# Sums of output weight blocks made in memory during attention, in a hybrid attention and gated-linear-attention block

## The chip, the cores and the metric

The kernel runs on one core of one Trainium2 chip. The metric is device time in microseconds (us). A core has TensorE (PE in the profile, with its weight loads as PEld), VectorE (DVE), ScalarE (ACT), GpSimd (POOL) and SyncE (SP); SP and POOL also issue DMAs, each on a queue of its own, and all DMAs run on the core's 16 DMA engines.

## What is computed

```python
h = rms_norm(x) * (1.0 + scale) + shift            # x: 512 x 2048, float32
proj = h @ w_in                                    # 2048 -> 7200 columns
aq, ak, av, ag, gq, gk, gv, gg, lr_f, lr_b = split(proj)
...                                                # dilated attention, 16 heads x 64, times silu(ag)
...                                                # gated linear attention, 4 heads, times silu(gg)
y = concatenate([a_out, g_out]) @ w_out            # 512 x 2048 @ 2048 x 2048
x = x + gate * y
return rms_norm(x) * final_gain
```

All is float32. A matrix product is made of three passes of TensorE on halves of each operand: a high half (rounded by ScalarE, lines 403 and 1094) and a low half (what is left, by VectorE, lines 389 and 1095); the passes are high x high, low x high and high x low (`three`, lines 213 to 215).

## The kernel before, in words

The work goes in stages. Up to about 188 us the condition vector, the normalised input and the first products are made. Then come ten "units", each a product of h with 512 columns of w_in in eight groups of 24 matmuls: qk2, qk4, qk6, gk, gv0, gv1, ag0, ag1, gg0, gg1. Each group's weights (128 x 1024, 512 KB) are loaded by SP into one of four `raw` buffers (`fetch`). Between a unit's matmuls stands other work, placed by a fraction of the unit: attention for two pairs of heads in each of qk2, qk4, qk6 and gk, the linear attention's heads in gv1, ag0, ag1 and gg0. A tile of attention goes from scores on TensorE (line 691) over VectorE, ScalarE and POOL (normalisation of p, line 703) back to TensorE (transposition, line 715). Where a pair of heads begins, parts of its keys (tiles ks and kl) are copied to the other half of the partitions by SP's DMAs (lines 664, 666); each head's bias (tile g) is loaded from memory too (line 679).

The order of TensorE's instructions is the program's. Those of the other engines are ordered, when the program is built, by a scheduler that takes what it holds ready, by priority; work placed between the matmuls has a raised priority. On the chip each engine's queue is in order: an instruction that waits holds those behind it.

The output projection multiplies by blocks in the manner of Winograd's form of Strassen: w_out's 2048 columns are taken as two pairs of 512-column halves (`OUT_PAIRS`), and each pair needs seven products of half size instead of eight, in the order P1, P7, P6, P4, P5, P3, P2. A product has four steps g of 12 matmuls, each with a 512 KB block of weights O0, O1, ... (28 for each pair, 56 in all). Four of the seven need sums (or with them sums of sums) of weight blocks: with blocks "11", "21", "12", "22", P7 takes T3 = 12 + 22, P6 takes T2 = 11 + 12 + 22, P4 takes T4 = T2 + 21, P5 takes T1 = 11 + 12. Before the change, `out_fetch` loads "12" into one of four `sum` tiles and has POOL issue an accumulating DMA that adds "22" from memory into it; after P7's use the same tile gets "11" added for P6, and after that "21" for P4. P5 loads a `raw` tile and adds to it. Weights are fetched two to four steps ahead. The operands' sums and halves are made beside it (`halves`, `to_s1` to `to_s4`), and `keep` and `add_up` take the products out.

Of the kernel before, what the change touches and what calls it, by code (L numbers as in the profile page):

```python
# [10 lines left out]
F32 = mybir.dt.float32  # L11
# [3 lines left out]
ALU = mybir.AluOpType  # L15
# [3 lines left out]
P = 128  # L19
# [60 lines left out]
def _runs():  # L80
# [6 lines left out]
    for j in range(2):  # L87
        cols = np.arange(512 * j, min(512 * j + 512, NREL))
        part = []
        for b, v in enumerate(seen):  # L90
            c = cols[bucket[cols] == v] - 512 * j
            if len(c):
# [24 lines left out]

OUT_ORDER = ("P1", "P7", "P6", "P4", "P5", "P3", "P2")
OUT_PAIRS = ((0, 1), (3, 2))
OUT_WEIGHTS = {"P1": ("11", None), "P7": ("12", "22"), "P6": (None, "11"), "P4": (None, "21"),  # L120
               "P5": ("11", "12"), "P3": ("22", None), "P2": ("21", None)}


def _plan(tasks, free, ready):
# [52 lines left out]
def block_kernel(ctx: ExitStack, tc: tile.TileContext, a: dict):  # L177
    nc = tc.nc
# [9 lines left out]
    dp = ctx.enter_context(tc.tile_pool(name="dp", bufs=1, space=DRAM))  # L188
# [8 lines left out]
    def PJ(name):  # L197
        return pp.tile([P, 512], F32, tag="pj", bufs=5, name=name)
# [13 lines left out]
    def three(ps, lh, ll, rh, rl, first, last, more=False):  # L212
        mm(ps, lh, rh, start=first, stop=False, skip_group_check=more)  # L213
        mm(ps, ll, rh, start=False, stop=False, skip_group_check=more)  # L214
        mm(ps, lh, rl, start=False, stop=last, skip_group_check=more)  # L215
# [27 lines left out]
    def RAW(name, shape):  # L243
        return wp.tile([P] + shape, F32, tag="raw", bufs=4, name=name)
# [100 lines left out]
    groups = [(u, g) for u in order for g in range(KT // 2)]  # L345
    groups += [("O", s) for s in range(2 * 4 * len(OUT_ORDER))]
    gi = {ug: i for i, ug in enumerate(groups)}
    raws, wts, low, sums_of = {}, {}, set(), {}

    def fetch(i):  # L350
        if i < len(groups) and i not in raws:
            u, g = groups[i]
            if u == "O":
                raws[i] = out_fetch(g)
            else:
                raws[i] = RAW(f"raw_{u}{g}", [2, 512])
                nc.sync.dma_start(raws[i], a["w_" + u][g])

    def out_fetch(s):

        pair, q = divmod(s, 4 * len(OUT_ORDER))
        prod, g = OUT_ORDER[q // 4], q % 4
        l, r = OUT_PAIRS[pair]
        block = {"11": (l, g), "21": (l, 4 + g), "12": (r, g), "22": (r, 4 + g)}
        load, add = OUT_WEIGHTS[prod]
        if load is None:
            t = sums_of[g]
        elif prod == "P7":
            t = sums_of[g] = op.tile([P, 2, 512], F32, tag="sum", bufs=4, name=f"sum{pair}{g}")
        else:  # L370
            t = RAW(f"raw_O{s}", [2, 512])
        if load is not None:
            j, z = block[load]
            nc.sync.dma_start(t, a[f"w_o{j}"][z])
        if add is not None:
            j, z = block[add]
            nc.gpsimd.dma_start(t, a[f"w_o{j}"][z], accum_op=ALU.add)  # L377
        return t

    def split(i):  # L380
        split_hi(i)
        split_lo(i)

    def split_lo(i):
        if i in raws and i not in low:
            u, g = groups[i]
            raw = raws[i].rearrange("p k c -> p (k c)")
            hi, lo = wts[i]
            tt(lo, raw, hi.bitcast(F32), op=ALU.subtract)
            low.add(i)  # L390

    def split_hi(i):
        if i < len(groups) and i not in wts:
            fetch(i)
            u, g = groups[i]
            raw = raws[i].rearrange("p k c -> p (k c)")
            dst = None
            if (u, g) == ("O", len(groups) - gi["O", 0] - 4):
                t = b8.tile([P, 2, 1024], F32R, tag="b8", name="wlast")
                dst = t[:, 0, :], t[:, 1, :]  # L400
            wts[i] = dst or (wp.tile([P, 1024], F32R, tag="whi", name=f"{u}{g}h"),
                             wp.tile([P, 1024], F32R, tag="wlo", name=f"{u}{g}l"))
            act(wts[i][0], raw, AF.Copy)
# [150 lines left out]
    for z in range(2):  # L554
        c = slice(512 * z, 512 * z + 512)
# [25 lines left out]
    n = len(chain) // 2  # L581
# [4 lines left out]
    for z in range(2):  # L586
        for e in range(3):
            name = ("mm", "a", 0, 7) if (z, e) == (1, 2) else ("m0", z, e)
# [3 lines left out]
    for i in range(n):  # L592
        if i > 7:
            mm_task(i)
        st, k, j = chain[i]
# [15 lines left out]
    for i in range(n, 2 * n):  # L611
        mm_task(i)
        st, k, j = chain[i]
# [3 lines left out]
    for w in range(4):  # L617
        for kt in range(4):
            j, g = w // 2 * 4 + kt, w % 2
# [342 lines left out]
    def urgent(go):  # L962
        with tc.high_priority(offset=20):
            go()

    spill = []

    def unit(name, natural, side=(), lr=None):
        side = sorted(spill + list(side), key=lambda x: x[0])
        spill[:] = [(at - 1, go) for at, go in side if at >= 1]  # L970
        side = [x for x in side if x[0] < 1]
        ps = [PJ(f"ps_{name}_{i}") for i in range(4)]
        pos, tick, ticks = 0, 0, 64
        for g in range(KT // 2):
            i0 = gi[name, g]
            split_hi(i0)
            split_hi(i0 + 1)
            for ahead in (2, 3):
                fetch(i0 + ahead)
            split_lo(i0)  # L980
            hi, lo = wts[i0]
            for i in range(4):
                for kk in range(2):
                    k = 2 * g + kk
                    rh, rl = h_hi[:, k, :], h_lo[:, k, :]
# [33 lines left out]
    for n, p in (("qk2", 0), ("qk4", 2), ("qk6", 4)):  # L1019
        ps = unit(n, False, attention((p, p + 1)) + ([(0.05, shift_row)] + some_sums(n) if p == 4 else []))  # L1020
        for q in range(2):
            qk_evict(p + 2 + q, ps[2 * q], ps[2 * q + 1])

    ps = unit("gk", False, attention((6, 7)) + some_sums("gk"))
    gla["k"] = B8("gkt", [4, 512])
    for i in range(4):
# [53 lines left out]
    def part(z, c):  # L1080

        return cat[z][:, :, half[c]]
# [6 lines left out]
    def halves(name, z, src):  # L1089

        hi, lo = (t[:, 4 * z:4 * z + 4, :] for t in ops[name])

        def go():
            act(hi, src, AF.Copy)
            tt(lo, src, hi.bitcast(F32), op=ALU.subtract)
        return go
# [4 lines left out]
    def diff(z):  # L1101
        d = gp.tile([P, 4, 256], F32, tag="g", name=f"diff{z}")
        tt(d, part(z, 0), part(z, 1), op=ALU.subtract)
        halves("S3", z, d)()

    def to_s1(z):
        tt(part(z, 1), part(2 + z, 1), part(z, 1), op=ALU.subtract)

    def to_s2(z):
        stt(part(z, 0), part(z, 1), -1.0, part(z, 0), op0=ALU.mult, op1=ALU.subtract)  # L1110

    def to_s4(z):
        tt(part(z, 0), part(2 + z, 0), part(z, 0), op=ALU.add)

    side = [(0.05, halves("A11", 0, part(0, 0))), (0.2, halves("A11", 1, part(1, 0))),
            (0.35, lambda: diff(0)), (0.5, lambda: diff(1)),
            (0.65, lambda: to_s1(0)), (0.8, lambda: to_s2(0))]
# [5 lines left out]
    op = ctx.enter_context(tc.tile_pool(name="op", bufs=1, reuse_waits="tile"))  # L1123
    for e in "hl":
        t = hp.tile([P, KT, 512], F32R, tag="h", name="c_" + e)
# [112 lines left out]
    def product(pair, prod, ps, first, last, rows=(0, 1)):  # L1238

        ah, al = ops[with_[prod]]  # L1240
        for g in range(4):
            s = (pair * len(OUT_ORDER) + OUT_ORDER.index(prod)) * 4 + g
            i0 = gi["O", s]
            ahead = 0 in rows
            if ahead:
                split_hi(i0)
                split_hi(i0 + 1)
                for n in (2, 3, 4):
                    fetch(i0 + n)
                split_lo(i0)  # L1250
                for go in todo.get((pair, prod, g), ()):
                    go()
            wh, wl = wts[i0]
            for n in rows:
                t = slice(P * n, P * n + P)
                for kk in range(2):
                    k = 2 * g + kk
                    c = slice(512 * kk, 512 * kk + 512)
                    three(ps[n], ah[:, k, t], al[:, k, t], wh[:, c], wl[:, c],
                          first and k == 0, last and k == 7, not first)  # L1260
                if ahead and n == 0:
                    split_lo(i0 + 1)
# [18 lines left out]
    for pair, (l, r) in enumerate(OUT_PAIRS):  # L1281
# [28 lines left out]
        s = [first_squares(n, [0, 1, r]) for n in range(2)]  # L1310
# [78 lines left out]
```

## Time and profile before

| | |
|---|---|
| median of 3 runs | 967.18 us (965.24 to 967.81) |
| profiled execution | 969.8 us, its span 968.0 us |
| mean granted TensorE clock | 0.984 |
| PE busy | 929.5 us (96%) |
| DVE, ACT, POOL busy | 656.0, 470.7, 85.7 us |
| attention (first scores to last tiles) | about 194 to 450 us |
| output projection (first matmul to last) | 768.7 to 958.4 us |
| read from and written to memory | 175.36 MB, 4.28 MB |

The rows of the profile name what an instruction writes and reads (out<-in), with its line; `sum<-in_w_o` is a load or an accumulating DMA of a weight block, `O4h` the high half of step 4's weights. A time of a wait is put to what came last. Slices are fortieths of the span, with busy shares in tenths.

### The profile page before, as it was taken

To read this page: it belongs to the slowest core of one execution; us is meant where nothing else is said; L and a number is where in the kernel's file an instruction comes from. 1 tells how busy PE (TensorE), PEld (TensorE's weight loads), DVE (VectorE), ACT (ScalarE), POOL (GpSimd) and SP (SyncE) were. 2 spreads that over 40 slices of the span, in tenths; PEclk is the share of its full clock that TensorE was granted. 3 is DMA by queue.
4 is the path that set the end of the run, shared out by engine and by line. 5 is a ranking of instruction groups with operands and counts; after the bars stand their busy time and mean duration, and the time that the engine had idled before them with its cause. 6 is when DMAs were issued, how large, how long until landed. Compare 5 with 4: busy or idle time off the path is not lost.

```text
span 968.0 us, 12067 instructions
## 1 busy us (share of the span) xinstructions
PE 929.5 (96%) x4375; PEld 763.7 (79%) x4375; DVE 656.0 (68%) x960; ACT 470.7 (49%) x770; POOL 85.7 (9%) x120
## 2 busy tenths in 40 slices
PE   8999999999999999999999999999999978898895
PEld 6888888888888888888778888888788855676684
DVE  8987999666665777666346575867875455594386
ACT  5543533655555556555135453635542444453464
POOL 0000000022121021120000000000100122102101
PEclk9999999999999999999999999999999989999898
DMA  9999596533432644534453353445444599979863
GB/s 354 401 413 374 198 349 228 157 117 104 128 104 75 196 156 136 162 107 142 145 170 112 107 167 134 156 156 170 152 153 138 174 265 250 270 249 242 173 200 148
DMA packets 51523, 184.62 MB, mean 191 GB/s; under 512 B 6436, under 2 KB 6724, under 8 KB 47240
## 3 DMA queue, kind: packets, MB, share of 16 engines
q1 hardware_dynamic: 46352, 166.44, 49.3%
q0 software_dynamic: 4672, 16.84, 8.9%
q8 instruction: 34, 0.56, 0.2%
q10 hardware_dynamic: 440, 0.57, 0.2%
q14 instruction: 25, 0.20, 0.1%
HBM read 175.36 MB, written 4.28 MB: 186 GB/s over the span
## 4 chain that ended last, share of the span: by engine, by line
PE 78%; DMA 9%; DVE 6%; issue 4%; ACT 2%; POOL 1%; SPq 0%; ACTq 0%; DVEq 0%; POOLq 0%
DMA sum<-in_w_o 5%; PE ps_qk L213 5%; PE ps_qk L215 5%; PE ps_qk L214 5%; PE o L729 3%; PE stb L215 3%; PE ps_gv L215 3%; PE ps_gv L214 3%; PE ps_gv L213 3%; PE stb L214 3%; PE t L715 3%; PE stb L213 3%; PE ps_ag L215 3%; PE ps_ag L213 3%; PE ps_ag L214 3%
## 5 line engine op out<-in xcount | busy, mean ns | idle before, releaser
L312 DVE CUSTOM_DVE_ANT_0 cb<-cb,sb,c_bcond 128x2048 f32<-128x2048 f32 (+1 forms) x32 | 73.4, 2294 | 1.0 <-DMA cb<-in_wm 0.6
L698 ACT ACTIVATE p<-p,st 128x512 f32<-128x512 f32 x64 | 46.1, 721 | 55.2 <-DVE st L695 54.8
L703 POOL TENSOR_SCALAR p<-p,st 128x512 f32<-128x512 f32 x62 | 43.0, 694 | 332.6 <-DVE st L699 283.8
L720 DVE TENSOR_TENSOR pt<-t,pt 128x512 fp32r<-128x512 f32 x64 | 43.7, 689 | 15.7 <-ACT pt L719 15.3
L695 DVE CUSTOM_DVE_ANT_0 p<-s,g 128x512 f32<-128x512 f32 x64 | 43.6, 687 | 15.2 <-PE s L692 14.9
L719 ACT ACTIVATE pt<-t 128x512 fp32r<-128x512 f32 x64 | 37.8, 591 | 9.7 <-PE t L715 8.6
L715 PEld LDWEIGHTS t<-c_ident,p 128*128 128x128 f32 x256 | 31.5, 140 | 9.7 <-POOL p L703 1.4
L715 PE MATMUL t<-c_ident,p 128*128 128x128 f32 x256 | 38.5, 273 | 0.1
L729 PEld LDWEIGHTS o<-pt,vv 128*128 128x128 f32 x256 | 34.8, 188 | 2.8
L729 PE MATMUL o<-pt,vv 128*128 128x256 f32 x256 | 35.6, 281 | 0.0
L312 DVE CUSTOM_DVE_ANT_0 rawg<-rawg,sb,gate 128x1024 f32<-128x1024 f32 x16 | 20.5, 1282 | 15.8 <-DMA rawg<-in_wg 15.7
L891 POOL TENSOR_SCALAR dc<-st,sc 128x256 f32<-128x256 f32 x16 | 8.5, 530 | 253.0 <-DVE st L888 248.1
L377 POOL DMA_DIRECT2D sum<-in_w_o x24 | 21.5, 919 | 67.4 <-DMA sum<-in_w_o 38.6
L699 DVE RECIPROCAL st<-st 128x1 f32<-128x1 f32 x64 | 10.3, 161 | 24.9 <-ACT p L698 24.9
L312 DVE CUSTOM_DVE_ANT_0 rawg<-rawg,sb,c_bcond 128x1024 f32<-128x1024 f32 x16 | 20.5, 1280 | 6.9 <-DMA rawg<-in_wg 6.9
L692 PE MATMUL s<-kl,qs 128*128 128x512 f32 x64 | 25.0, 391 | 0.0
L691 PE MATMUL s<-ks,qs 128*128 128x512 f32 x64 | 25.0, 390 | 0.0
L898 ACT ACTIVATE sq<-st,sc 128x256 f32<-128x256 f32 x24 | 12.2, 507 | 18.6 <-DVE st L888 10.4
L732 ACT ACTIVATE oh<-o 64x256 f32<-64x256 f32 x32 | 12.2, 381 | 14.4 <-PE o L729 13.4
L312 DVE CUSTOM_DVE_ANT_0 rawv<-rawv,shb,vbias 128x1024 f32<-128x1024 f32 x8 | 10.6, 1324 | 12.6 <-DMA rawv<-in_wv 12.6
L736 DVE TENSOR_TENSOR cat<-o,oh 64x256 f32<-64x256 f32 x32 | 13.3, 416 | 8.2 <-ACT oh L732 7.8
L467 ACT ACTIVATE h_hi<-xt,shift 128x512 fp32r<-128x512 f32 x16 | 11.5, 719 | 13.0 <-DVE shift L312 13.0
(1520 smaller groups left out, 2984.1 us busy)
## 6 DMA issues: line engine op xcount, KB each, us to landing
cb<-in_wm SPq DMA_DIRECT2D x31, 1024.0 KB, 8.9
rawg<-in_wg SPq DMA_DIRECT2D x32, 512.0 KB, 3.3
raw_O<-in_w_o SPq DMA_DIRECT2D x32, 512.0 KB, 4.8
raw_qk<-in_w_qk SPq DMA_DIRECT2D x24, 512.0 KB, 3.3
sum<-in_w_o POOLq DMA_DIRECT2D x24, 512.0 KB, 11.9
rawb<-in_w_sb SPq DMA_DIRECT2D x16, 512.0 KB, 5.4
rawv<-in_wv SPq DMA_DIRECT2D x16, 512.0 KB, 4.0
raw_gv<-in_w_gv SPq DMA_DIRECT2D x16, 512.0 KB, 3.3
```

Source lines behind the costliest of these rows:

```text
L213: mm(ps, lh, rh, start=first, stop=False, skip_group_check=more)
L214: mm(ps, ll, rh, start=False, stop=False, skip_group_check=more)
L215: mm(ps, lh, rl, start=False, stop=last, skip_group_check=more)
L312: nc.vector.tensor_tensor_reduce(out=w, in0=w, in1=with_, op0=ALU.mult, op1=ALU.add, scale=1.0, scalar=init, accum_out=dst)
L691: mm(ps, qs[:, q], ks, start=True, stop=False)
L695: nc.vector.tensor_tensor_reduce(out=t, in0=ps, in1=gt[h][:, P * i:P * i + 512], op0=ALU.add, op1=ALU.min, scale=1.0, scalar=3e38, accum_o ...
L698: act(t, t, AF.Exp, bias=st[:, 0:1], scale=-1.0, accum_out=st[:, 1:2])
L703: nc.gpsimd.tensor_scalar(t, t, st[:, 2:3], 1.0, op0=ALU.mult, op1=ALU.mult)
L715: nc.tensor.transpose(pk[:, kt * P:kt * P + P], t[:, kt * P:kt * P + P], ident)
L719: act(hi, src, AF.Copy)
L720: tt(lo, src, hi.bitcast(F32), op=ALU.subtract)
L729: mm(po[:, :256], vv[h // 4][:, kt, h % 4, :], t[:, w, kt, :], start=kt == 0 and w == 0, stop=kt == 3 and w == 1)
```

## The change

The sums are made in memory. For each pair and step g there are four tiles of 512 KB in memory: T1, T3, T2 and T4 (`OUT_SUMS`). Each is made by a copy from memory to memory, issued by SP (`sum_start`: a block of w_out, or T1 for T2, or T2 for T4), and an accumulating DMA, issued by POOL (`sum_add`), that adds another block in memory: 32 copies and 32 adds in 64 rows of 8 KB. A copy of T2 or T4 waits for the add that finishes its source, and an add waits for its copy. `block_sums` hands the 64 operations out to the ten units by `SUM_OPS_IN`, in the order of a pipeline of six stages, placed evenly in each unit with raised priority.

The output projection then loads every block plainly: 56 loads by SP, none by POOL. The four `sum` tiles are gone; odd steps from 7 on use three buffers of their own, the others the four `raw` buffers, and loads are fetched two to five steps ahead.

```diff
-OUT_WEIGHTS = {"P1": ("11", None), "P7": ("12", "22"), "P6": (None, "11"), "P4": (None, "21"),
-               "P5": ("11", "12"), "P3": ("22", None), "P2": ("21", None)}
+OUT_WEIGHTS = {"P1": "11", "P7": "T3", "P6": "T2", "P4": "T4", "P5": "T1", "P3": "22", "P2": "21"}
+OUT_SUMS = {"T1": ("11", "12"), "T3": ("12", "22"), "T2": ("T1", "22"), "T4": ("T2", "21")}
+OUT_DEEP = 6
+SUM_OPS_IN = {"qk2": 7, "qk4": 7, "qk6": 7, "gk": 7, "gv0": 5, "gv1": 7, "ag0": 7, "ag1": 6, "gg0": 6, "gg1": 5}
...
     def out_fetch(s):
...
-        if load is None:
-            t = sums_of[g]
-        elif prod == "P7":
-            t = sums_of[g] = op.tile([P, 2, 512], F32, tag="sum", bufs=4, name=f"sum{pair}{g}")
+        if s % 2 and s >= OUT_DEEP:
+            t = op.tile([P, 2, 512], F32, tag="raw", bufs=3, name=f"raw_O{s}")
         else:
             t = RAW(f"raw_O{s}", [2, 512])
-        if load is not None:
-            j, z = block[load]
-            nc.sync.dma_start(t, a[f"w_o{j}"][z])
-        if add is not None:
-            j, z = block[add]
-            nc.gpsimd.dma_start(t, a[f"w_o{j}"][z], accum_op=ALU.add)
+        if what in OUT_SUMS:
+            d = dsum[pair, what, g]
+            nc.sync.dma_start(t.rearrange("p k c -> p (k c)"),
+                              bass.AP(d.tensor, d.offset, [[1024, P], [1, 1024]]))
+        else:
+            nc.sync.dma_start(t, out_block(pair, what, g))
         return t
...
+    def flat(t):
+        return bass.AP(t.tensor, t.offset, [[2048, 64], [1, 2048]])
+
+    def sum_start(pair, name, g):
+        def go():
+            src = OUT_SUMS[name][0]
+            dsum[pair, name, g] = t = dp.tile([64, 2048], F32, tag=f"{name}{pair}{g}", name=f"{name}{pair}{g}")
+            nc.sync.dma_start(t, flat(dsum[pair, src, g] if src in OUT_SUMS else out_block(pair, src, g)))
+        return go
+
+    def sum_add(pair, name, g):
+        def go():
+            nc.gpsimd.dma_start(dsum[pair, name, g], flat(out_block(pair, OUT_SUMS[name][1], g)), accum_op=ALU.add, max_dma_last_dim=8192)
+        return go
+
+    sum_ops = []
+    for s in range(13):
+        for lag, fn, name in ((0, sum_start, "T1"), (0, sum_start, "T3"), (1, sum_add, "T1"), (1, sum_add, "T3"),
+                              (2, sum_start, "T2"), (3, sum_add, "T2"), (4, sum_start, "T4"), (5, sum_add, "T4")):
+            if 0 <= s - lag < 8:
+                sum_ops.append(fn(*[((s - lag) // 4), name, (s - lag) % 4]))
+
+    def block_sums(name):
+        n = SUM_OPS_IN[name]
+        r = [sum_ops.pop(0) for _ in range(n)]
+        return [((q + 0.5) / n, x) for q, x in enumerate(r)]
...
-        side = sorted(spill + list(side), key=lambda x: x[0])
+        side = sorted(spill + list(side) + block_sums(name), key=lambda x: x[0])
...
-                for n in (2, 3, 4):
+                for n in (2, 3, 4, 5):
                     fetch(i0 + n)
```

TensorE's instructions and their order are the same. Three places show how the others stand now. The first is SP's queue in the unit qk2, where weights of the next unit (raw_qk4..), the heads' biases (g2 to g5) and, now, the copies are issued; a name such as T201 is sum T2 of pair 0, step 1. Before:

```order
L679 DMA g2_1706<-grow_149 128x896
L357 DMA raw_qk41_1983<-in_w_qk4 128x1024
L679 DMA g3_1846<-grow_149 128x896
L357 DMA raw_qk42_2067<-in_w_qk4 128x1024
L357 DMA raw_qk43_2173<-in_w_qk4 128x1024
L679 DMA g4_2164<-grow_149 128x896
```

and now:

```order
L711 DMA g2_1712<-grow_149 128x896
L392 DMA T200_2472<-T100_1554 16x8192
L392 DMA T103_2583<-in_w_o0 16x8192
L359 DMA raw_qk41_1992<-in_w_qk4 128x1024
L392 DMA T303_2679<-in_w_o1 16x8192
L711 DMA g3_1854<-grow_149 128x896
L392 DMA T201_2942<-T101_1707 16x8192
L359 DMA raw_qk42_2077<-in_w_qk4 128x1024
L392 DMA T110_3148<-in_w_o3 16x8192
L392 DMA T310_3259<-in_w_o2 16x8192
L359 DMA raw_qk43_2185<-in_w_qk4 128x1024
L711 DMA g4_2176<-grow_149 128x896
```

Six copies stand between loads that followed each other; T200 and T201 read what an add has finished, so SP waits for it there, with the loads behind. The second place is POOL in the same unit, where the probabilities of each tile (p10 is tile 0 of head 1) are normalised. Before:

```order
L703 TENSOR_SCALAR p10_1668<-p10_1668,st10_1669 128x512
L703 TENSOR_SCALAR p11_1711<-p11_1711,st11_1712 128x512
L703 TENSOR_SCALAR p12_1739<-p12_1739,st12_1740 128x512
L703 TENSOR_SCALAR p13_1780<-p13_1780,st13_1781 128x512
L703 TENSOR_SCALAR p20_1802<-p20_1802,st20_1803 128x512
```

and now:

```order
L735 TENSOR_SCALAR p10_1672<-p10_1672,st10_1673 128x512
L397 DMA T302_2215<-in_w_o1 64x2048
L735 TENSOR_SCALAR p11_1717<-p11_1717,st11_1718 128x512
L397 DMA T200_2472<-in_w_o1 64x2048
L735 TENSOR_SCALAR p12_1745<-p12_1745,st12_1746 128x512
L397 DMA T103_2583<-in_w_o1 64x2048
L735 TENSOR_SCALAR p13_1786<-p13_1786,st13_1787 128x512
L397 DMA T303_2679<-in_w_o1 64x2048
L735 TENSOR_SCALAR p20_1808<-p20_1808,st20_1809 128x512
```

An accumulating DMA now stands ahead of nearly every normalisation, and waits for its copy to land. By the order all 64 operations are in the attention units: the first copy stands before the first bias g0, the last, of T413, before the load of qk66, and its add before p90, though the code hands them out up to gg1. The third place is SP's queue at the start of the output projection. Before:

```order
L374 DMA raw_O2_6404<-in_w_o0 128x1024
L374 DMA raw_O3_6462<-in_w_o0 128x1024
L374 DMA raw_O16_6715<-in_w_o0 128x1024
L374 DMA raw_O17_6736<-in_w_o0 128x1024
L374 DMA sum00_6464<-in_w_o1 128x1024
L374 DMA sum01_6485<-in_w_o1 128x1024
L1137 DMA garow_6492<-gatet_6490 16x128
L374 DMA sum02_6511<-in_w_o1 128x1024
```

and now:

```order
L380 DMA raw_O2_6499<-in_w_o0 128x1024
L380 DMA raw_O3_6558<-in_w_o0 128x1024
L377 DMA raw_O4_6560<-T300_1610 128x1024
L377 DMA raw_O5_6562<-T301_1814 128x1024
L377 DMA raw_O7_6607<-T303_2679 128x1024
L1169 DMA garow_6588<-gatet_6586 16x128
L377 DMA raw_O9_6651<-T201_2942 128x1024
L377 DMA raw_O6_6582<-T302_2215 128x1024
```

Where two loads for P5 stood early and the sums' first parts followed, the finished sums T3 (for O4 to O7) and T2 (O8 on) are loaded in their turn.

More of the change, by code (lines that the diff above doesn't have):

```diff
@@ L347, in block_kernel @@
     gi = {ug: i for i, ug in enumerate(groups)}
-    raws, wts, low, sums_of = {}, {}, set(), {}
+    raws, wts, low = {}, {}, set()
     def fetch(i):
@@ L357, in fetch, with out_block @@
                 nc.sync.dma_start(raws[i], a["w_" + u][g])
+    def out_block(pair, which, g):
+        l, r = OUT_PAIRS[pair]
+        j, z = {"11": (l, g), "21": (l, 4 + g), "12": (r, g), "22": (r, 4 + g)}[which]
+        return a[f"w_o{j}"][z]
     def out_fetch(s):
         pair, q = divmod(s, 4 * len(OUT_ORDER))
[L362 to L365, printed above, removed]
@@ L366, in out_fetch @@
-        if load is None:
-            t = sums_of[g]
-        elif prod == "P7":
-            t = sums_of[g] = op.tile([P, 2, 512], F32, tag="sum", bufs=4, name=f"sum{pair}{g}")
+        what, g = OUT_WEIGHTS[OUT_ORDER[q // 4]], q % 4
+        if s % 2 and s >= OUT_DEEP:
+            t = op.tile([P, 2, 512], F32, tag="raw", bufs=3, name=f"raw_O{s}")
         else:
             t = RAW(f"raw_O{s}", [2, 512])
-        if load is not None:
-            j, z = block[load]
-            nc.sync.dma_start(t, a[f"w_o{j}"][z])
@@ L375, in out_fetch @@
-        if add is not None:
-            j, z = block[add]
-            nc.gpsimd.dma_start(t, a[f"w_o{j}"][z], accum_op=ALU.add)
-        return t
+        if what in OUT_SUMS:
[4 more added lines that the diff above has]
+            nc.sync.dma_start(t, out_block(pair, what, g))
+        return t
+    dsum = {}
+    def flat(t):
+        return bass.AP(t.tensor, t.offset, [[2048, 64], [1, 2048]])
```

## Prediction

> **What bounds the kernel now.** I read the page's slices first, then the busy time by stretches, then TensorE's matmuls of the output projection, then the waits and the chain.
>
> ```profile
> span 968.0 us, 12067 instructions
> PE   8999999999999999999999999999999978898895
> PEclk9999999999999999999999999999999989999898
> DMA  9999596533432644534453353445444599979863
> ```
>
> TensorE is full from the second slice to the 32nd; then the output projection shows gaps and a lower granted clock, with the DMA engines full. The stretches below give start:end, PE, PEld, DVE, ACT and POOL busy, then the clock, the DMA share and GB/s.
>
> ```profile
> 168.00:204.00 36.00, 36.00 (x165) 29.80 (x164) 25.69 (x45) 22.51 (x40) 2.07 (x3) 1.00 0.53 151
> 204.00:250.00 46.00, 45.98 (x253) 38.71 (x252) 28.50 (x66) 26.09 (x53) 9.02 (x13) 1.00 0.29 100
> 250.00:264.00 14.00, 14.00 (x71) 11.88 (x70) 10.07 (x18) 7.74 (x14) 0.00 (x0) 1.00 0.53 148
> 264.00:314.00 50.00, 50.00 (x274) 42.29 (x273) 29.72 (x69) 27.77 (x56) 10.42 (x15) 1.00 0.27 90
> 314.00:342.00 28.00, 27.98 (x144) 23.25 (x143) 20.55 (x40) 15.90 (x31) 3.47 (x5) 1.00 0.66 215
> 768.00:834.40 66.40, 52.88 (x198) 37.96 (x196) 36.90 (x33) 31.30 (x37) 15.63 (x18) 0.92 1.01 263
> ```
>
> From 168 to 342, most of attention, TensorE never waits and the DMA engines have room; from 768 to 834 it is the reverse. The waits (who, for whom, total, times, longest) and three steps of the chain say for what:
>
> ```profile
> PE gx L213 <- ACT O4h L403: 4.8, 1, 4.8
> PE gx L213 <- ACT O14h L403: 3.8, 1, 3.8
> PE g L215 <- DVE O55l L389: 1.8, 1, 1.8
> 784.60 11.33 DMA sum<-in_w_o
> 809.18 16.04 DMA sum<-in_w_o
> 887.13 16.28 DMA sum<-in_w_o
> sum<-in_w_o POOLq DMA_DIRECT2D x24, 512.0 KB, 11.9
> raw_O<-in_w_o SPq DMA_DIRECT2D x32, 512.0 KB, 4.8
> ```
>
> TensorE waits for ScalarE's high half, ScalarE for a sum tile, and this for an accumulating DMA: 11.9 us from issue to landing, a plain load 4.8. The third row (O55) is a wait for VectorE, in the last product.
>
> **Removed: the waits for sums.** The first matmuls of each product, with the first and last start of the four:
>
> ```profile
> L213 PE MATMUL g<-O0h,A11h x4: 389/389/389, 768.7 to 770.7; 128*128 128x512 f32 x4
> L213 PE MATMUL gx<-O4h,S3h x4: 628/628/792, 785.1 to 789.5; 128*128 128x512 f32 x4
> L213 PE MATMUL g<-O8h,c_h x4: 389/391/395, 800.8 to 803.5; 128*128 128x512 f32 x4
> L213 PE MATMUL gx<-O12h,c_h x4: 389/395/500, 815.0 to 818.0; 128*128 128x512 f32 x4
> L213 PE MATMUL g<-O16h,c_h x4: 389/389/389, 834.4 to 836.4; 128*128 128x512 f32 x4
> L213 PE MATMUL gx<-O32h,S3h x4: 389/389/389, 878.9 to 881.0; 128*128 128x512 f32 x4
> L213 PE MATMUL g<-O36h,c_h x4: 628/628/794, 893.7 to 898.1; 128*128 128x512 f32 x4
> L213 PE MATMUL gx<-O40h,c_h x4: 389/389/389, 912.6 to 914.7; 128*128 128x512 f32 x4
> L213 PE MATMUL g<-O48h,c_h x4: 389/389/389, 934.4 to 936.4; 128*128 128x512 f32 x4
> ```
>
> From O40 to O48 eight steps take 21.8 us, so a full-speed step takes 2.725 and a product of four 10.9. What each product took above this: O0 to O4 16.4 - 10.9 = 5.5; to O8 4.8; to O12 3.3; to O16 8.5; in the second pair O32 to O36 3.9 and to O40 8.0. The sum is **34.0 us**, slow matmuls after a wait (628 ns for 389) included. It all lies on TensorE's path. O16 to O32 takes 44.5 for 43.6, so 0.9 stays, as no sum causes it.
>
> What is late next there? Loads: a step takes 0.52 MB per 2.725 us, 192 GB/s, with 56 plain loads for 40; the DMA engines carried 263 from 768 to 834 while they also added, and seven buffers with loads five steps ahead (13.6 us) cover 4.8. That POOL no longer issues adds there frees an engine for which nobody waits. VectorE:
>
> ```profile
> 777.18 3.49 DVE L1095 TENSOR_TENSOR c_l<-cat,c_h 128x1024 fp32r<-128x1024 f32 x3
> ```
>
> Three in 3.49 us, 1.16 each. O0 to O16 needs some 30 of these on VectorE (16 low halves of weights, ten of operands, four sums of operands): 35 us beside 43.6 of TensorE. So it is close but not the bound, and I take all 34.0.
>
> **Added: 32 copies and 32 adds in memory.** By the order all stand in the attention units, though the code hands them out over ten units: the last copy is issued before the load of qk66, the last add before p90. So the 174 us from 168 to 342 must carry them. Their price:
>
> ```profile
> q1 hardware_dynamic: 46352, 166.44, 49.3%
> q0 software_dynamic: 4672, 16.84, 8.9%
> ```
>
> POOL's queue q0 is nearly all 32 adds: 8.9% of 968 is 86.2 us, 2.69 per add. Its sums lie in SBUF; no row shows one in memory. SP's q1 moves 166.44 MB in 477 us, 349 GB/s: 0.524 MB is 1.50 us. No row copies memory to memory either. Bounds: copy from 1.50 (writing hides behind reading) to 3.0 (both counted); add from 2.69 to 2.69 + 1.50 = 4.2. I take the lower ends, nearest to the rows, since every load there also reads and writes at once.
>
> The Trainium skill, "Collectives: The Full Stack", section "The bandwidth ceiling", says that a reduce by DMA is half as fast as a copy because it reads two sources; 195 GB/s for q0 beside 349 agrees roughly, and by it memory as the target costs an add nothing more, which is the low end.
>
> The densest place is 204 to 250, where 13 copies and 13 adds now stand. SP's own: 0.29 x 46 = 13.3, plus 13 x 1.50 = 32.8 us; POOL's 13 x 2.69 = 35.0. Each queue alone fits in 46, both together (67.8) do not: something is up to 22 us late by 250, less at 264, as no copies stand between. From 264 to 314 it is 13.5 + 13 x 1.50 + 12 x 2.69 = 65 in 50. What can be late at no cost? The adds themselves, first needed at 768, except where a copy of T2 or T4 on SP waits for the add that it reads; in SP's order that copy stands some 10 us or more behind. The loads:
>
> ```profile
> 189.60 0.46 SPq L666 DMA_DIRECT2D kl<-kl  x1
> kl<-kl SPq DMA_DIRECT2D x16, 128.0 KB, 3.1
> 194.16 0.39 PE L691 MATMUL s<-ks,qs 128*128 128x512 f32 x1
> 190.99 0.45 SPq L357 DMA_DIRECT2D raw_qk<-in_w_qk  x1
> L403 ACT ACTIVATE qk26h<-raw_qk x1: 1049/1049/1049, 218.8 to 218.8; 128x1024 fp32r<-128x1024 f32 x1
> 252.07 0.47 SPq L666 DMA_DIRECT2D kl<-kl  x1
> 260.50 0.39 PE L691 MATMUL s<-ks,qs 128*128 128x512 f32 x1
> 205.49 0.69 POOL L703 TENSOR_SCALAR p<-p,st 128x512 f32<-128x512 f32 x1 [1.71 <-DVE st L699]
> 210.16 0.60 PE L715 MATMUL t<-c_ident,p 128*128 128x128 f32 x4
> ```
>
> A weight load (qk26) has 218.8 - 191.0, nearly 28 us to landing and use. The key copies are tight: in the first unit 194.16 - 189.60 - 3.1 = 1.5 us, in the second 260.50 - 252.07 - 3.1 = 5.3. An add also takes POOL's turn (it waits for its copy to land; behind it stands the next normalisation of p, for which TensorE's transposition waits): p03 ends at 206.2, its use is 210.16, 4.0 us of cover. So I expect three small stalls, one where each pair of heads begins, of 1 to 2 us, as long as a copy or add in the way: **5 us**. Bounds: 0, if all lateness falls on the adds; above, the third rival. A gain there is excluded: TensorE is full.
>
> The gate units (342 on) keep their DMAs and order, so 0.
>
> **The sum.** The profiled execution took 969.8 us (span 968.0 and 1.8 around it). 969.8 - 34.0 + 5 = 940.8. It lies 2.6 above the median of the runs, 967.2; less that, **938.2 us**. About 0.3%, 2.9 us, is what a measurement of this kernel can tell from no change.
>
> **Rivals.**
> *Partly given back (0.13).* The queues' lateness reaches the key copies and POOL's turns in full: half of 22 us at 250 less 5.3, and half of 15 at 314 less 5.3, some 8, with two or three turns of POOL late by 4 us each: 15 to 30 us in all. 948 to 963. For it: both queues overfull. Against: 14 quiet us behind each dense part.
>
> *VectorE takes over (0.07).* 35 of 43.6 us is an average; if its order puts operand work ahead of low halves, half of the first pair's 22.1 us comes back: 949. For: the third product alone has ten such operations, 11.6 us beside 10.9. Against: three weight buffers to run ahead.
>
> *Memory is slow, and attention becomes the bound (0.20): slower.* At 3.0 a copy and 4.2 an add, SP alone needs 13.3 + 39 = 52.3 of 46. Up to 264 come 7.4 more of its own and 13 x 4.2 = 54.6 of adds: 114 in 60, 54 late; from 264 to 342, 32 + 15 x 3.0 + 15 x 4.2 = 140 in 78, 62 late. SP runs in order, so weight loads stand behind it: less 28 us of cover, 26 and 34, 60 us. 938.2 - 5 + 60 = 993. It decides from a lateness of 28 + 17 = 45 per unit (34 lost in both), near a copy of 2.5 and an add of 3.7. For it: no row shows memory as a target. Against: loads at 349 GB/s write as they read.
>
> The Trainium skill, "DMA: Bandwidth & Descriptors", "Latency and other measured facts", gives about 210 GB/s per direction for copies between tensors in HBM; by it a copy takes an estimated 2.5 us, which is about that point. No run shown has one.
>
> **How the numbers follow.** The forecast has 0.60 and its own range is 930 to 950: from no cost, with the 0.9 and O55's 1.8 us gone too (969.8 - 36.7 - 2.6 = 930.5), to 12 us more of cost than I take. With the first two rivals it reaches 963, and with the near part of the third 972; beyond lie some 0.18. So 930 to 972. Faster: 0.60 + 0.09 + 0.05 = 0.74; same 0.04; slower 0.20 + 0.02 = 0.22.
>
> **What would show it.** Right: O4, O8, O12, O36 and O40 follow 10.9 us after the product before; no wait for sums; TensorE's busy time from 168 to 342 within 5 us of full; q0 below 15%. Wrong: waits of TensorE for p, ks or kl in attention, a copy far over 1.5 us, SP waiting for adds, or gaps after 768 released by VectorE.

## The result, and the profile after

The changed kernel takes 955.56 us (median of 4 runs, 953.65 to 955.92), the kernel before 967.11 beside it. The ratio is 0.988 with a 95% interval of 0.986 to 0.990: faster by 11.6 us, where 29 were forecast. The profiled execution took 955.7 us, span 953.9, against 969.8 and 968.0.

First the slices of the changed kernel's page, TensorE, its granted clock and the DMA engines:

```profile
span 953.9 us, 12126 instructions
PE   8999999989899979999999999999999999999996
PEclk9999999989999989999999999999999999999998
DMA  9999496979999998353245425355455446966853
```

The gaps of the output projection, at the right, are gone, and new ones stand in slices 9, 11 and 15, in attention, where the DMA engines, at 2 to 6 tenths before, are now at 7 to 9 or more. What was gained at the end is seen in the first matmuls of its products (first and last start of the four):

```profile
L215 PE MATMUL g<-O0h,A11h x4: 389/389/389, 791.7 to 793.7; 128*128 128x512 f32 x4
L215 PE MATMUL gx<-O4h,S3h x4: 389/389/389, 803.2 to 805.2; 128*128 128x512 f32 x4
L215 PE MATMUL g<-O16h,c_h x4: 389/389/389, 835.8 to 837.8; 128*128 128x512 f32 x4
L215 PE MATMUL gx<-O32h,S3h x4: 389/389/389, 879.3 to 881.4; 128*128 128x512 f32 x4
L215 PE MATMUL g<-O36h,c_h x4: 389/389/389, 890.2 to 892.2; 128*128 128x512 f32 x4
L215 PE MATMUL gx<-O40h,c_h x4: 389/389/389, 901.1 to 903.1; 128*128 128x512 f32 x4
```

O0 to O16 takes 44.1 us, where it took 65.7 (768.7 to 834.4), and O32 to O40 21.8 for 33.7. All matmuls shown last 389 ns; none is slow after a wait. But O0 starts at 791.7, 23.0 us later than before: the end moved by 14.1 in the profiled executions (969.8 to 955.7), so the stage from O0 on is shorter by 37.1.

Where the 23.0 were lost: the first matmuls of four units, here in the changed kernel,

```profile
L215 PE MATMUL ps_qk<-h_hi,qk20h x8: 389/389/389, 188.6 to 193.3; 128*128 128x512 f32 x8
L215 PE MATMUL ps_qk<-h_hi,qk40h x8: 389/389/396, 267.0 to 272.7; 128*128 128x512 f32 x8
L215 PE MATMUL ps_qk<-h_hi,qk60h x8: 387/389/482, 337.4 to 343.3; 128*128 128x512 f32 x8
L215 PE MATMUL ps_gk<-h_hi,gk0h x8: 389/389/396, 412.7 to 418.4; 128*128 128x512 f32 x8
```

and here in a kernel without any of the sum DMAs (the first experiment below):

```profile
L215 PE MATMUL ps_qk<-h_hi,qk20h x8: 389/389/389, 188.2 to 193.0; 128*128 128x512 f32 x8
L215 PE MATMUL ps_qk<-h_hi,qk40h x8: 389/389/396, 253.5 to 259.3; 128*128 128x512 f32 x8
L215 PE MATMUL ps_qk<-h_hi,qk60h x8: 387/389/482, 319.9 to 325.8; 128*128 128x512 f32 x8
L215 PE MATMUL ps_gk<-h_hi,gk0h x8: 389/389/396, 386.4 to 392.1; 128*128 128x512 f32 x8
```

The second is the time table of an undisturbed attention. Against it qk2 takes 13.1 us more (78.4 for 65.3), qk4 4.0, qk6 8.8; with 0.4 ahead of qk2 that is 26.3 us. Later units lose nothing: from gk0 to O0 the changed kernel takes 379.0 us and the kernel before took 382.5, which is why O0 is only 23.0 late. The stretches of the changed kernel (start:end, PE, PEld, DVE, ACT and POOL busy, clock, DMA share, GB/s) say how:

```profile
168.00:204.00 36.00, 31.66 (x130) 25.76 (x129) 22.98 (x38) 19.62 (x36) 3.75 (x5) 0.92 0.95 262
204.00:250.00 46.00, 44.53 (x235) 36.99 (x234) 25.01 (x58) 23.42 (x48) 14.73 (x21) 0.99 0.89 273
250.00:264.00 14.00, 11.95 (x57) 9.58 (x56) 8.03 (x15) 7.08 (x13) 5.78 (x7) 0.88 0.95 255
264.00:314.00 50.00, 46.78 (x244) 38.82 (x243) 28.03 (x59) 25.37 (x49) 13.69 (x19) 1.00 1.02 286
314.00:342.00 28.00, 27.90 (x153) 23.34 (x152) 20.10 (x38) 17.16 (x33) 8.63 (x12) 1.00 1.01 291
342.00:450.00 108.00, 101.62 (x523) 84.46 (x522) 69.70 (x148) 54.03 (x106) 19.70 (x27) 0.97 0.61 187
```

And so do its waits (who, for whom, total, times, longest):

```profile
PE s L723 <- DMA ks<-ks: 7.5, 3, 4.3
PE t L747 <- POOL p L735: 5.3, 4, 1.9
PE s L724 <- DMA kl<-kl: 4.3, 1, 4.3
```

TensorE stands idle 17.6 us (282 less the six busy times) where it stood 0.1 before, nearly all of it for key copies (11.8) and for normalised probabilities (5.3). And it pays twice: idle, it loses its clock. In the timeline of TensorE (start, duration, what, idle time before):

```profile
194.44 0.39 PE L217 MATMUL ps_qk<-h_lo,qk21h 128*128 128x512 f32 x1
199.18 0.76 PE L723 MATMUL s<-ks,qs 128*128 128x512 f32 x1 [4.34 <-DMA ks<-ks]
199.74 0.63 PE L724 MATMUL s<-kl,qs 128*128 128x512 f32 x1
...
204.86 0.41 PE L215 MATMUL ps_qk<-h_hi,qk21h 128*128 128x512 f32 x1
```

One wait of 4.3 us is followed by 5.7 us (199.18 to 204.86) of matmuls of 0.63 us each in the place of 0.39. These 13 matmuls start 0.43 us apart where those ahead of the wait start 0.23 apart, so the slow clock adds some 2.7 us to the wait. For the whole of attention, busy time by what the clock lacks (31.66 x 0.08, 44.53 x 0.01, 11.95 x 0.12, 101.62 x 0.03) gives an estimate of 7.5 us; with the 17.6 idle that is about 25 of the 26.3.

The key copies are late because each takes longer to land. In the DMA view (KB each, median us from issue to landing), first before the change, then after it:

```profile
ks<-ks SPq DMA_DIRECT2D x16, 128.0 KB, 2.2
```

```profile
ks<-ks SPq DMA_DIRECT2D x16, 128.0 KB, 9.5
```

POOL's queue q0 (packets, MB, share of 16 engines) took 9.1% of 953.9, 86.8 us for 32 adds, **2.71** each:

```profile
q0 software_dynamic: 2624, 16.84, 9.1%
```

### The profile page after: what moved, and what is told of

Same layout as the page of the kernel before. It is cut to its first block, busy times and chain, and to the rows that moved or that the text cites. A ratio compares the mean times of both kernels' runs of the same rounds, so it can differ in the third digit from the quotient of the medians.

```text
span 953.9 us, 12126 instructions
## 1 busy us (share of the span) xinstructions
PE 922.7 (97%) x4375; PEld 763.3 (80%) x4375; DVE 656.1 (69%) x960; ACT 473.3 (50%) x770; POOL 84.5 (9%) x120
## 4 chain that ended last, share of the span: by engine, by line
PE 56%; DVE 3%; DMA 1%; issue 1%; ACT 1%; ACTq 0%; DVEq 0%
PE g L217 4%; PE g L216 4%; PE g L215 4%; PE ps_gv L217 3%; PE ps_gv L216 3%; PE ps_gv L215 3%; PE ps_ag L215 3%; PE ps_ag L217 3%; PE ps_ag L216 3%; PE ps_gg L215 2%; PE ps_gg L216 2%; PE ps_gg L217 2%; PE o L761 2%; PE ps_gk L217 2%; PE ps_gk L215 2%; PE ps_gk L216 2%
## 5 line engine op out<-in xcount | busy, mean ns | idle before, releaser
L735 POOL TENSOR_SCALAR p<-p,st 128x512 f32<-128x512 f32 x62 | 49.3, 808 | 129.3 <-DVE st L731 99.0
L397 POOL DMA_DIRECT2D T<-in_w_o x32 | 25.6, 800 | 202.5 <-DMA T<-in_w_o 131.5
L731 DVE RECIPROCAL st<-st 128x1 f32<-128x1 f32 x64 | 10.3, 161 | 24.8 <-ACT p L730 24.8
L1246 POOL TENSOR_SCALAR x<-x,rn 128x512 f32<-128x512 f32 x3 | 3.4, 1137 | 216.6 <-ACT rn L1235 216.6
L723 PEld LDWEIGHTS s<-ks,qs 128*128 128x128 f32 x64 | 12.4, 194 | 12.0 <-issue 7.1
L314 DVE CUSTOM_DVE_ANT_0 rawv<-rawv,shb,vbias 128x1024 f32<-128x1024 f32 x8 | 10.2, 1281 | 12.7 <-DMA rawv<-in_wv 12.6
```

The lines of the kernel that those rows point to most:

```text
L314: nc.vector.tensor_tensor_reduce(out=w, in0=w, in1=with_, op0=ALU.mult, op1=ALU.add, scale=1.0, scalar=init, accum_out=dst)
L723: mm(ps, qs[:, q], ks, start=True, stop=False)
L735: nc.gpsimd.tensor_scalar(t, t, st[:, 2:3], 1.0, op0=ALU.mult, op1=ALU.mult)
```

## The experiments

Three theories of the 26 us stood at the outset. One queue (A1): small transfers stand behind large copies in SP's own queue. Full engines (A2, later W): the DMA work of the stretch exceeds what the engines can carry. Order (B, later O): an add on POOL waits for its copy, and the normalisation of p waits behind it. Each kernel is the changed one with the edit shown; 955.6 is the time to compare with. The kernel before took 966.5 to 967.1 beside them.

**No sums at all.**

```diff
 def out_fetch(s):
+        what = OUT_SUMS[what][1] if what in OUT_SUMS else what
 def block_sums(name):
-        r = [sum_ops.pop(0) for _ in range(n)]
-        return [((q + 0.5) / n, x) for q, x in enumerate(r)]
+        return []
```

> Left out: all 64 DMAs that make the sums in memory, copies and adds; the output projection loads single blocks in the place of sums, so its products are of other data. Its own 56 loads, their order and all other work stay. Theory A (the 26.4 us that attention lost are the price of the sum DMAs there): O0 starts again near 765 as all of the loss is gone, 955.7 - 26.4 = 929 us. Rival R (the loss comes from the rest of the change, its other buffers and the deeper prefetch, or from a lower clock of the attention units): attention stays as slow, 950 to 956 us.

Measured: 930.10 us (929.43 to 930.26; ratio to before 0.962, 0.960 to 0.964). The sum DMAs cost 955.6 - 930.1 = 25.5 us. The rest of the change shows no cost in attention: gk begins at 386.4 here and at 386.2 in the kernel before. So 930 is what an arrangement of the sums that hides them wholly would take, and it is called the floor below.

**No adds, copies kept.**

```diff
-            nc.gpsimd.dma_start(dsum[pair, name, g], flat(...), accum_op=ALU.add, max_dma_last_dim=8192)
+            pass
```

> Left out: the 32 accumulating DMAs on POOL's queue; the 32 copies on SP's queue stay, so the sums lack their second block. Theory A1 (one queue: key copies and loads are late because they stand behind sum copies on SP's own queue): the copies stay where they were, so most of the loss stays, 945 to 953 us. Theory A2 (full engines: copies and adds together ask for more than the DMA engines have, 68 us of work in 46): without adds SP's 33 of 46 fit, waits for ks, kl and p are gone, 929 to 934 us. Rival B (POOL's turns: an add that waits for its copy holds the normalisation of p behind it): only the waits for p go, some 5 to 8 us, 947 to 951 us.

Measured: 930.18 us (929.78 to 930.40). All 32 copies on SP's queue, without the adds, cost nothing. A2 had this (929 to 934); A1 in its simple form (945 to 953) falls, and so does B as the whole cause (947 to 951). The rows of SP's queue q1 (packets, MB, share of 16 engines), first without the copies (span 928.5), then with them (928.2), give their price:

```profile
q1 hardware_dynamic: 48656, 174.83, 54.3%
```

```profile
q1 hardware_dynamic: 49680, 191.61, 59.6%
```

59.6% of 928.2 less 54.3% of 928.5 is 49.0 us for 32: **1.53 us** a copy, 1.50 by the prediction. The Trainium skill's "DMA: Bandwidth & Descriptors", section "Latency and other measured facts", by whose 210 GB/s a copy was estimated at 2.5 us, gives its 207 to 214 GB/s for tiles with rows of 16 KB that lie far apart in memory. The figure does not carry over to these contiguous blocks: 0.524 MB in 1.53 us is 343 GB/s. And the key copies land as fast as before:

```profile
ks<-ks SPq DMA_DIRECT2D x16, 128.0 KB, 2.3
```

**Key copies on ScalarE's queue.**

```diff
-            nc.sync.dma_start(ks[oth].bitcast(F32), ks[own].bitcast(F32))
+            nc.scalar.dma_start(ks[oth].bitcast(F32), ks[own].bitcast(F32))
-            nc.sync.dma_start(kl[oth].bitcast(F32), kl[own].bitcast(F32))
+            nc.scalar.dma_start(kl[oth].bitcast(F32), kl[own].bitcast(F32))
```

> The copies of ks and kl from one half of the partitions to the other are issued by ScalarE on its own DMA queue instead of SP's; nothing else changes. A1 (one queue): they no longer stand behind copies and loads of 512 KB, land in 2 to 4 us as before the change, the waits of TensorE for ks and kl (11.8 us) and the slow matmuls after them go: 938 to 943 us. A2 (full engines: whatever queue a small transfer is in, each of the 16 engines serves the big ones too): landing stays above 6 us and the time within 3 us of the changed kernel's, 952 to 957 us, or longer if ScalarE gets to the issue late.

Measured: 969.52 us (968.46 to 973.37; ratio to before 1.004, 1.002 to 1.006): 14 us worse than the changed kernel, above both forecasts (938 to 943, 952 to 957). The landing of a key copy in the DMA view:

```profile
ks<-ks ACTq DMA_DIRECT2D x16, 128.0 KB, 7.1
```

TensorE's waits in attention:

```profile
PE t L747 <- POOL p L735: 15.7, 6, 4.6
PE s L724 <- DMA kl<-kl: 4.4, 2, 2.6
PE s L723 <- DMA ks<-ks: 3.5, 2, 3.1
```

The adds on POOL, with the first and last start:

```profile
L397 POOL DMA_DIRECT2D T<-in_w_o x32: 769/784/965, 172.7 to 335.8; - x32
```

In a queue of its own a key copy still needs 7.1 us, with the DMA engines' share at 1.01 to 1.02 from 204 to 342: not SP's queue alone, but the engines themselves are full. And SP, which in the changed kernel stood at the key copies waiting for ScalarE, now runs ahead. There, of SP's waits and of the adds:

```profile
SPq L696 <- ACT ks L695: 15.8, 7, 5.3
```

```profile
L397 POOL DMA_DIRECT2D T<-in_w_o x32: 762/782/1068, 173.5 to 367.1; - x32
```

The last add goes out at 335.8 in the place of 367.1, though attention got longer. The waits for keys shrink from 11.8 to 7.9 us; those for p grow from 5.3 to 15.7. The three longest of these (4.5, 4.6 and 3.5 us) each end right behind an add at which POOL had stood 7.7 to 8.2 us for the copy of a T2 or T4 (T<-T), so with full engines the order does pass the lateness on to p. The same DMA work, sooner, costs more. That the lost wait is the reason fits these rows, but it was not tried by itself. ScalarE, too, now stands 10.2 us (5.9 and 4.3) behind key copies in its queue, which it did not before, and how much of the 14 us that makes is open.

**Copies held behind the weight loads.** What the table of ten units says is made true: a copy may not be issued ahead of the newest weight load.

```diff
-                nc.sync.dma_start(raws[i], a["w_" + u][g])
+                newest[:] = [nc.sync.dma_start(raws[i], a["w_" + u][g]).ins]
...
-            nc.sync.dma_start(t, flat(...))
+            with tc.issue_after(newest[0]):
+                nc.sync.dma_start(t, flat(...))
```

> Each sum copy is held in the issue order behind the weight load that the code issued last before it, so the 32 copies and, through the add's wait for its copy, the 32 adds are spread over the ten units that the table names, some 14 pairs in attention instead of 32. A (the density in attention is the price): 68 us of DMA work in 46 becomes some 35, the waits for ks, kl and p shrink to 0 to 8 us in all, and the gate units with their share of 0.61 take the rest at no cost: 930 to 938 us. Rival G (each pair costs some 0.8 us of TensorE wherever it stands, 26.4 over 32): 950 to 957 us.

Measured: **936.11 us** (934.05 to 938.41; ratio to before 0.968, 0.967 to 0.970). It beats both kernels, by 19.5 and 30.4 us. Its adds (L398 there) go out from 179.9 to 741.9, and transfers land sooner:

```profile
L398 POOL DMA_DIRECT2D T<-in_w_o x32: 770/782/826, 179.9 to 741.9; - x32
```

```profile
T<-in_w_o POOLq DMA_DIRECT2D x32, 512.0 KB, 6.8
ks<-ks SPq DMA_DIRECT2D x16, 128.0 KB, 3.6
```

The same 64 transfers cost 6.0 us above the floor when spread over 560 us, 25.5 in some 195 (173.5 to 367.1). A price per transfer wherever it stands (rival G of this run) is out.

**Held, and the gate units alone.** As above, with none in attention.

```diff
-SUM_OPS_IN = {"qk2": 7, "qk4": 7, "qk6": 7, "gk": 7, "gv0": 5, "gv1": 7, "ag0": 7, "ag1": 6, "gg0": 6, "gg1": 5}
+SUM_OPS_IN = {"qk2": 0, "qk4": 0, "qk6": 0, "gk": 0, "gv0": 10, "gv1": 11, "ag0": 11, "ag1": 11, "gg0": 11, "gg1": 10}
```

> As with the held copies, each sum copy stays behind the newest weight load, and the table hands the 64 steps to the six units from gv0 to gg1 alone, 10 or 11 each; attention has none. A (price is density beside attention): attention runs as before the change (O0 some 20 us earlier than in the changed kernel), gv0 to gg1 need 0.44 x 320 = 140 us of DMA work of their own plus 32 x 1.5 + 32 x 2.7 = 134, which is 274 in 320: 929 to 934 us. Rival G (the gate units stall once their DMA share nears 0.85, as loads of weights then come late): 936 to 945 us.

Measured: 943.23 us (941.03 to 946.32), as this run's own rival G (the gate units stall) had it. Attention is undisturbed, and the gate units lose 13 us. Their stretches, then the longest waits of TensorE and of VectorE, then the landing of the loads that VectorE waits for:

```profile
450.00:600.00 150.00, 146.53 (x692) 120.28 (x691) 76.33 (x100) 57.73 (x95) 16.49 (x24) 1.00 0.81 239
600.00:768.00 168.00, 160.08 (x769) 134.66 (x768) 109.40 (x147) 74.00 (x111) 18.08 (x23) 0.97 0.79 239
```

```profile
PE kt L902 <- DVE ki L892: 7.9, 2, 4.1
DVE rawg L314 <- DMA rawg<-in_wg: 58.9, 18, 6.4
```

```profile
rawg<-in_wg SPq DMA_DIRECT2D x32, 512.0 KB, 5.7
```

These units have a chain of their own that depends on short landings: VectorE takes `rawg` loads one after another, and with a landing of 5.7 us for 3.3 (the kernel without sums) it waits 58.9 us for them, 20.7 there. Ahead of the wait of TensorE for ki that ends at 637.2, for one, VectorE had stood 3.5 and 1.3 us for `rawg` before it made ki. That all of the 13 us comes about so is not shown. The engines need not be full all the time for it: the mean share of 0.8 was enough, but it hides swings from 0.44 to 1.08 between windows of 6 us (560 to 740).

**A plain copy for the add.** The DMA on POOL's queue moves its block and does not add.

```diff
-            nc.gpsimd.dma_start(dsum[pair, name, g], flat(...), accum_op=ALU.add, max_dma_last_dim=8192)
+            nc.gpsimd.dma_start(dsum[pair, name, g], flat(...), max_dma_last_dim=8192)
```

> The 32 DMAs on POOL's queue copy their block over the first one and do not add, so that the sums in memory hold one block alone; place, queue, waits and sizes stay. Theory W (the total of DMA work in attention is the bound): 2.05 to 2.7 us for an add becomes about 1.5 for a copy, the work from 168 to 342 falls from some 200 us to 72 + 32 x 1.5 + 32 x 1.5 = 168 in 174, and most of the loss goes: 932 to 940 us. Theory O (the order is the price: DMAs on POOL that wait for their copy, between the normalisations of p, whatever they cost on the engines): 948 to 956 us.

Measured: 930.80 us (929.91 to 930.97), 0.7 above the floor, a little below W's range (932 to 940) and far from O's (948 to 956). The waits, the places and the bytes named in the program are the same. A stretch of attention shows TensorE full beside nearly full DMA engines:

```profile
204.00:250.00 46.00, 45.98 (x253) 38.73 (x252) 28.42 (x66) 26.13 (x53) 15.48 (x26) 1.00 0.93 342
```

The price is another:

```profile
q0 software_dynamic: 2624, 16.84, 4.9%
```

4.9% of 929.0 is 45.5 us, **1.42** each; so an add, at 2.71, costs 1.9 of them. The Trainium skill's "Collectives: The Full Stack", section "The bandwidth ceiling", with its reduce at half the speed of a copy, agrees. And DMAs that wait on POOL ahead of p, 16 of them behind a T2 or T4, hurt nobody when the engines have time for them: theory O falls as a cause by itself. Why the packets of an add take longer is not shown by these runs.

**Half the adds.** Every add of an odd step is left out.

```diff
+            if g % 2 == 0:
                 nc.gpsimd.dma_start(dsum[pair, name, g], ...)
```

> Left out: every second add (16 of 32; the sums of two of four blocks lack their second block). All copies stay, and the order. Theory W (a total that must fit: 72 us of other work from 168 to 342, 43 of copies, 2.7 for an add): 72 + 43 + 16 x 2.7 = 158 in 174 fits, and nearly all of the loss goes: 930 to 934 us. Theory P (each add costs its 0.8 us of TensorE wherever it stands): half of 25, 940 to 945 us.

Measured: 932.62 us (931.61 to 932.87): 2.5 above the floor, where half of 25.5 would be 12.8. Half the adds cost a tenth of what all of them cost. This is a threshold, as W had it (930 to 934), and not a price for each (940 to 945).

**Smaller rows, and later adds.** Two kernels that move the same work at the same place in another form. The first has rows of 2 KB:

```diff
-..., accum_op=ALU.add, max_dma_last_dim=8192)
+..., accum_op=ALU.add, max_dma_last_dim=2048)
```

> The adds move rows of 2 KB in the place of 8 KB, with the same bytes. Theory F (small transfers are late because they take turns with packets of 8 KB): key copies land in 5 to 7 us in the place of 9.5, the waits for ks and kl halve: 946 to 951 us. Theory W (the total of work is the bound): smaller rows can only raise the price of an add, 955 to 975 us; q0 takes more than 9.1% of the span.

Measured: 952.40 us (951.40 to 955.39). Key copies land in 6.5 us, as theory F had it, and the waits for them nearly vanish, yet the time falls by 3.2 only, between the two forecasts (946 to 951, 955 to 975), and the runs' ranges overlap with the changed kernel's; p is late instead, and an add costs more (10.1% of 953.6 by 32 is 3.0 us):

```profile
ks<-ks SPq DMA_DIRECT2D x16, 128.0 KB, 6.5
```

```profile
PE s L723 <- DMA ks<-ks: 1.3, 1, 1.3
PE t L747 <- POOL p L735: 13.1, 6, 3.6
```

```profile
q0 software_dynamic: 8768, 16.84, 10.1%
```

The Trainium skill's "DMA: Bandwidth & Descriptors", section "Queues, rings and completion order", says that each DMA engine takes turns between queues packet by packet. The shorter landing beside smaller rows (6.5 us for 9.5) agrees with that; the 7.1 us that remained for key copies in a queue of their own do not speak against it.

The second puts each add three steps behind its copy instead of one, and the next copy of a chain two behind that add:

```diff
-    for s in range(13):
-        for lag, ... in ((0, sum_start, "T1"), (0, sum_start, "T3"), (1, sum_add, "T1"), (1, sum_add, "T3"),
-                         (2, sum_start, "T2"), (3, sum_add, "T2"), (4, sum_start, "T4"), (5, sum_add, "T4")):
+    for s in range(21):
+        for lag, ... in ((0, sum_start, "T1"), (0, sum_start, "T3"), (3, sum_add, "T1"), (3, sum_add, "T3"),
+                         (5, sum_start, "T2"), (8, sum_add, "T2"), (10, sum_start, "T4"), (13, sum_add, "T4")):
```

> The list of sum steps is drawn apart: an add follows its copy three steps later in the place of one, the next copy of a chain two after that; the same 64 steps in the same places of the attention units. Theory O (POOL's turns: an add stands waiting for its copy and the normalisation of p behind it): the copy has landed when its add's turn comes, the waits of TensorE for p (5.3 us) and the lower clock after them go: 945 to 951 us. Theory W (total of DMA work): the adds start sooner one after another, the engines stay full, key copies stay late: 953 to 960 us.

Measured: 952.07 us (950.65 to 955.47), between the two forecasts and not apart from the changed kernel's by much (3.5 us, the runs' ranges overlap). The waits for p did not go (6.3 us for 5.3); those for keys fell to 7.0 from 11.8. Rearranged inside the same stretch, the lateness moves between keys and p.

**Two attempts on the last 6 us.** The first has held copies and the later adds; the second is the same with a table of 8, 8, 8, 0, 10, 8, 6, 6, 5, 5.

> The held copies over ten units, and each add three steps behind its copy. The held kernel (936.1) lost some 1 us in qk2 and 4.8 in gk, with POOL waiting 194.6 us in all for copies. Theory O (what is left is POOL standing at an add whose copy has not landed, with a normalisation of p behind it): 930 to 933 us. Theory W (what is left comes of the DMA work in gk, 0.67 of the engines and the loads in bursts): 935 to 938 us.

> The held copies, adds three steps behind, and a table that gives gk none and fewer to ag and gg: 8, 8, 8, 0, 10, 8, 6, 6, 5, 5. Theory W: the loss of gk (4.8 us) goes, qk2 to qk6 stay under 0.9 of the engines, gv0 took 10 at no cost before: 930 to 933 us. Rival: what leaves gk stalls gv1 or qk4 as much: 935 to 938 us.

Measured: 939.88 (939.65 to 941.09) and 937.10 (936.75 to 937.73). The first is slower than held alone and above both of its forecasts (930 to 933, 935 to 938); the second is no better than held alone, as its rival had it, though the stall moved to qk6 and not to gv1 or qk4. By the first matmuls of the units, gk takes 71.4 us in the held kernel, 71.1 and 67.1 in these two (66.3 without sums). So later adds did not help gk, which speaks against O again, and ag1 took 4.7 us more; the table did help gk, and qk6 took 4.9 us more for that. How the last 6 us are to be had stays open.

## Why the prediction was wrong

The range (930 to 972) holds the result and the sign was right; the size was not: 11.6 of 29 us. The forecast's own range, 930 to 950, does not hold 955.6; the wide one does because of the rivals.

*Removed, 34.0 us: right.* The products follow each other by 10.9 us (the first of them takes 11.5), no wait for sums is left, loads keep up and VectorE holds nothing up. The stage gave 37.1; the 3.1 above the forecast are mainly the two waits put aside as staying, 0.9 in O16 to O32 (43.5 now) and O55's 1.8.

*Prices: right.* A copy 1.53 us for 1.50, an add 2.71 for 2.69, memory as the target costs nothing extra. The rival in which memory is slow falls on that. The prices are not constants, though: in the held kernel q0's 10.3% of 934.0 us makes 3.0 an add, and in the changed kernel q1 took only 39.5 us more than without sums (57.0% of 953.9 less 504.2), 1.2 a copy. So the sums of engine time below are estimates, good to some ten us.

*Gate units, 0: nearly right.* gg0 even got rid of a 2.0 us wait (kt for ki): gk0 to O0 takes 379.0 for 382.5. Why that went was not tried; the kernel without sums has it too (379.9).

*Added, three small stalls, 5 us: this term was mis-sized; it was 26.3.* The step that failed is the sentence that a stall is "as long as a copy or add in the way". The prediction added up two pieces of the stretch, found 22 and 15 us too much work, and let the excess fall on adds that nobody awaits until 768. It never made the sum over all of 168 to 342 at these prices, which its own rows allowed: the kernel's own work there is 0.53 x 36 + 0.29 x 46 + 0.53 x 14 + 0.27 x 50 + 0.66 x 28 = 71.8 us, the copies 48, the adds 86.1, together **206 in 174**. A backlog of 32 us has no quiet place in the stretch to be worked off, and the engines serve everyone slowly meanwhile: a key copy with 1.5 us of cover lands 7.3 us later (9.5 for 2.2), not later by one transfer. TensorE's busy time from 168 to 342, named as the mark, is 162.8 of 174. Nor could the adds slide out: an add stands ahead of nearly every normalisation of p on POOL, so p, and TensorE with it, waits until the adds are under way. In the changed kernel POOL stands 8.1 us for a copy ahead of the add at 238.98, and TensorE's wait for p that ends at 240.54 follows; with the key copies on ScalarE's queue the same made the three longest waits. The experiments show the threshold on both sides, with no run between: 72 + 49 + 45 = 166 us of work with plain copies costs 0.7 us, about as much with half the adds 2.5, and 72 + 49 + 87 = 208 costs 25.5. The same adds and copies spread over ten units cost 6.0. Past the threshold the total does not set the price: with the key copies on another queue it was 39.4 (969.5 - 930.1).

*The rival "partly given back" (948 to 963, 0.13) is what happened,* by its own mechanism: lateness of keys and of POOL's turns. It held 8 us for the keys, measured 11.8, and two or three turns of POOL, measured four with 5.3 us. What it lacked is the clock, some 7.5 us more.

## What to carry to other kernels

Where work for the DMA engines is moved into a stretch that looks free, add up the engine time of everything in that stretch, as far as the order lets it spread and no further, and compare the total with its length. If it doesn't fit, expect the excess on whatever has the least cover: here it came back on small key copies, in a queue of their own too, and on p, and not only on the adds, which had time. A table that names units for an operation means nothing if the order lets it run ahead: holding each copy behind a load it should follow was worth 19.5 us here.

## What the chip showed that was not expected

A wait costs more than its length: 4.3 us of idle TensorE were followed by 5.7 us of matmuls at 0.63 us for 0.39, so 17.6 us of waits in attention cost some 25. Plain copies filled the engines to 0.93 of a stretch of attention, at 342 GB/s, with a loss of 0.7 us in all, while in the gate units a mean of 0.8 with adds lost 13. So the share alone does not tell how full the engines may be; that the cover of the transfers beside decides it is likely and not shown. And freeing SP of a wait (the key copies on another queue) made the kernel 14 us slower; the adds then went out sooner, which fits a wait that had held them back, but ScalarE stood behind key copies too, and no run tried either alone.
